# Layer two's residual: LayerNorm scale and offset applied by GpSimd during the input projection and kept in DRAM, in a two-layer RWKV-7 / MLA / gMLP step on Trainium2

## The chip, the cores and the metric

The kernel runs on one core of one Trainium2 chip. The metric is the device time of one execution in microseconds (us). The time before is the median of three executions; the profile is of one more execution.

## What is computed

One inference step of a backbone of two post-norm layers over 1152 tokens (1024 latent, 128 context), width 1024. Cut to what matters here:

```python
for layer in (0, 1):
    h   = x * (1 + scale1) + shift1                  # modulated input
    z   = h @ w_in                                   # input projection: RWKV | MLA (q, kv, rope) | gMLP
    y   = concat(rwkv7(z), mla(z), gmlp(z))
    mix = y @ w_out
    x   = layer_norm(ALPHA * x + gate1 * mix, ln1_g, ln1_b)       # the residual ALPHA * x
    ff  = swiglu(x * (1 + scale2) + shift2, ffn_w_in, ffn_w_out)
    x   = layer_norm(ALPHA * x + gate2 * ff, ln2_g, ln2_b)
```

`layer_norm` is `(x - mean) * rsqrt(var + eps) * g + b`. At the end of layer one the kernel stores only the normalised rows, without `ln2_g` and `ln2_b`. Where layer two needs `ALPHA * x` as its residual, it has to put both back: `xhat * (ALPHA * ln2_g) + ALPHA * ln2_b`. That pair of operations is what the change is about.

## The kernel before

Tokens are nine tiles of 128 rows (`NT` = 9), and three blocks of 384 columns where tokens run along the free dimension. Every fp32 product is three matmuls of split operands (high by high, high by low, low by high; `mm3`, L115 to L121), so each operand is split into a high and a low tile (`split`, L125 and L126; weights in `split_w`, L321 and L324). The Tile framework puts the instructions into an order for each engine and adds the waits: a tile of a pool that takes memory which an earlier pool had waits for whatever still uses that memory. Engines and DMA queues work strictly in their order. DMAs are issued from three queues: SP (`nc.sync`), ACT (`nc.scalar`) and POOL (`nc.gpsimd`).

A layer goes through these stages (`run`, L1515):

1. `project_a` (L344, called at L1541): the 416 columns of `w_in` that MLA reads. Each of the nine token tiles takes 24 matmuls (L360) into one PSUM bank of stream `ps`, which has four banks (`streams`, L1539). A finished bank is copied to a row tile `zrow` and stored to the DRAM tensor `zA`. The pool `zr` with `zrow` opens on the left side just before, and closes just after.
2. `mla_prep` (L579, called at L1549): loads `zA` back as `zt` (L602, SP queue, three buffers), takes RMS norms (ACT L605 and L606, DVE L607 to L613), the rope products on GpSimd (L623 to L626), and transposes on TensorE (L629, L630).
3. The other projections, gMLP, attention and the RWKV scan.
4. `w_out` (L1330): for each tile four products with a quarter of `w_out` (evicted by DVE with the gate, L1352), then `finish` (L1354): the residual is loaded to `xres` (L1363, ACT queue), added to `z` (L1366), normalised (L1304), transposed and modulated to the FFN's input (`to_h`, L284: TensorE L295, ACT L299, DVE L301), then given LN1's scale and offset on GpSimd (L1369, L1370; the last two tiles on DVE) and stored.
5. `ffn` (L1390): first products evicted at L1417 and L1418. Its last part adds the FFN's output to `acc` (GpSimd, L1485), normalises (L1318) and stores the rows as the DRAM tensor that the next layer reads as `self.x` (ACT queue, L1500). At the end of layer one it also makes the modulated input of layer two (`to_h`), the last tiles of which overlap `project_a` of layer two.

Eviction and store in `project_a`, the copy that alternates between ACT and DVE, and the scale and offset rows that `ln_rows` broadcasts to 128 partitions:

```python
            for b in g:
                for j, p in enumerate(ps[b]):
                    z = self.t(tmp, [128, 416], "zrow", bufs=2)
                    self.copy(z, p)                                  # L131 ACT, L133 DVE
                    nc.scalar.dma_start(self.zA[3 * b + j], z)       # L387
...
        gb = self.t(pool, [128, 2, D], tag, bufs=bufs)
        for x, n in enumerate("gb"):                                 # L1299: two DMAs, POOL queue
            nc.gpsimd.dma_start(gb[:, x], self.I[f"{name}_{n}"][l:l + 1].to_broadcast([128, D]))
        if factor is not None:                                       # L1301
            nc.gpsimd.tensor_scalar(gb, gb, factor, None, op0=ALU.mult)
```

In layer two's `w_out`, L1335 makes the rows ALPHA * ln2_g and ALPHA * ln2_b (tile `lnprev`), and `finish` multiplies and adds them on DVE, in place on `xres` (L1364, L1365). Layer one's `w_out` has neither.

Of the kernel before, what the change touches and what calls it, by code (L numbers as in the profile page):

```python
# [11 lines left out]
ALU = mybir.AluOpType  # L12
# [4 lines left out]
D = 1024  # L17
# [4 lines left out]
NT = T // 128  # L22
# [6 lines left out]
ALPHA = (2 * DEPTH) ** 0.25  # L29
# [49 lines left out]
class Net:  # L79
# [1250 lines left out]
    def w_out(self, l, lnp, y, ws, gate, cols, wp):  # L1330

        nc = self.nc
        zp, close_z = self.pool("z", "right")
        gb = self.ln_rows(l, "ln1", zp)
        gp = None if l == 0 else self.ln_rows(l - 1, "ln2", zp, ALPHA, "lnprev")  # L1335
        x1 = self.t(self.dram, [NT, 128, D], "x1", bufs=1)
        self.h2 = {}
        zs = {}

        def product(i, ns):  # L1340
            if i == 8:
                gates.append(self.gate(l, 0, 1, lnp))
            if i not in zs:
                zs[i] = self.t(zp, [128, D], "z", bufs=3) if i % 4 else self.t(wp, [128, D], "z0")
            hh, hl = y[i // 3]
            s = slice(128 * (i % 3), 128 * (i % 3) + 128)
            for n in ns:
                wh, wl = ws[n]
                w = slice(256 * n, 256 * n + 256)
                p = self.psum()  # L1350
                self.mm3(p[:, 0:256], [(hh[:, k, s], hl[:, k, s], wh[:, k], wl[:, k]) for k in (6, 7, 0, 1, 2, 3, 4, 5)])
                nc.vector.tensor_tensor(zs[i][:, w], p[:, 0:256], gates[-1][:, w], op=ALU.mult)  # L1352

        def finish(i):  # L1354
            if i % 3 == 0:
                self.h2[i // 3] = self.hy()
            z = zs[i]
            x = self.t(lnp, [128, D], "xres")
            if l == 0:
                nc.scalar.dma_start(x, self.x_tile(i))  # L1360
                nc.vector.scalar_tensor_tensor(z, x, ALPHA, z, op0=ALU.mult, op1=ALU.add)
            else:
                nc.scalar.dma_start(x, self.x[i])  # L1363
                nc.vector.tensor_tensor(x, x, gp[:, 0], op=ALU.mult)  # L1364
                nc.vector.tensor_tensor(x, x, gp[:, 1], op=ALU.add)  # L1365
                nc.vector.tensor_tensor(z, z, x, op=ALU.add)  # L1366
            self.normalise(z, lnp)
            self.to_h(i, z, self.h2[i // 3], cols, lnp, eng=nc.vector, act=True)
            (nc.vector if i > 6 else nc.gpsimd).tensor_tensor(z, z, gb[:, 0], op=ALU.mult)  # L1369
            (nc.vector if i > 6 else nc.gpsimd).tensor_tensor(z, z, gb[:, 1], op=ALU.add)  # L1370
            nc.scalar.dma_start(x1[i], z)
        gates = [gate]

        for i in range(3):
            product(i, range(3))
        for i in range(NT):
            product(i, [3] if i < 3 else range(4))
            finish(i)
        close_z()
        self.x = x1  # L1380
# [134 lines left out]
    def run(self):  # L1515
        nc = self.nc
# [5 lines left out]
        xp, close = self.pool("x0", "right")  # L1522
# [14 lines left out]
                self.to_h(i, xs[i], self.h[i // 3], self.mod_cols(0, 0), xp, 6, (4 * e,) if g[0] == 0 else (0, 4))  # L1537
        for l in range(self.depth):
            self.streams(ps="0123", bg="67", mp="45")  # L1539
            zp, close_z = self.pool("zr", "left")  # L1540
            self.project_a(l, zp, *(() if l else (first_ada, rows)))  # L1541
            close_z()
# [69 lines left out]
            xp, close_x = self.pool("wx", "right")  # L1612
# [61 lines left out]
```

## Time and profile before

| | |
|---|---|
| three executions | 3696.85, 3701.43, 3705.38 us; median 3701.43 us |
| profiled execution, its own time | 3698.82 us (span 3697.0 us) |
| TensorE (PE) busy | 3486.4 us, 94% of the span |
| VectorE (DVE) busy | 1881.7 us, 51% |
| GpSimd (POOL) busy | 1436.8 us, 39% |
| ScalarE (ACT) busy | 1099.0 us, 30% |
| mean granted clock of TensorE | 0.968 |

PE is TensorE's matmuls, PEld its weight loads, SP the engine that only issues DMAs. ACTq, SPq and POOLq are an engine's issuing of DMAs. Times of the trace are microseconds from the start of the span. A name such as `zrow<-b` is "tile written <- tile read", with buffer numbers left out; `b` is a PSUM bank. An arrow in brackets names what ended the engine's idle time before that row. The chain of waits is the chain of work that ended last, followed back from the last instruction. Idle time of an engine that is not on that chain costs nothing.

### The profile page before, as it was taken

Reading aid. Unit: us, or ns where it says so; the run is one execution under the profiler, and the core shown is the slowest. Engines: PE = TensorE matmul, PEld = TensorE weight load, DVE = VectorE, ACT = ScalarE, POOL = GpSimd, SP = SyncE. Lnnn points to the kernel's source line nnn. Section 1 sums busy time; section 2 is a strip of 40 time slices with the busy share of each in tenths; the row PEclk is TensorE's granted clock in tenths of the full one; section 3 lists DMA queues with packets and bytes.
Section 4 is the critical chain, followed back from the end, with each engine's and each line's share of the span. In section 5 each row is a group of like instructions: output and inputs, shape, how many; then the busy total and the mean of one; then the engine's idle time right before and its main releaser. Section 6 shows DMA issues by size and latency. Waiting matters only on the chain.

```text
span 3697.0 us, 61363 instructions
## 1 busy us (share of the span) xinstructions
PE 3486.4 (94%) x25199; PEld 3030.5 (82%) x25199; DVE 1881.7 (51%) x3064; ACT 1099.0 (30%) x2156; POOL 1436.8 (39%) x1315
## 2 busy tenths in 40 slices
PE   8999789997999999999999997999988999999997
PEld 6888566776988888988989895777778999999996
DVE  3554676755733333333465457767458233433357
ACT  3443344333411111111144434544334211111111
POOL 2324677664411111111453247766634111111146
PEclk9999799998999999999999998989999999999998
DMA  7566545435232222212234654644343111111122
GB/s 288 164 205 171 121 103 135 87 77 167 104 97 91 80 80 80 69 58 69 100 110 118 206 148 106 134 104 96 80 163 110 46 35 46 46 35 46 46 86 80
DMA packets 462584, 387.11 MB, mean 105 GB/s; under 512 B 170412, under 2 KB 394024, under 8 KB 461088
## 3 DMA queue, kind: packets, MB, share of 16 engines
q1 hardware_dynamic: 371744, 249.12, 23.8%
q10 hardware_dynamic: 82176, 113.70, 10.0%
q0 software_dynamic: 8384, 20.38, 1.9%
q8 instruction: 198, 3.24, 0.4%
q14 instruction: 82, 0.67, 0.1%
HBM read 280.10 MB, written 103.02 MB: 104 GB/s over the span
## 4 chain that ended last, share of the span: by engine, by line
PE 72%; DVE 11%; DMA 7%; POOL 4%; issue 3%; ACT 2%; SPq 1%; ACTq 0%; POOLq 0%; DVEq 0%
PE b L119 19%; PE b L121 19%; PE b L120 19%; PE b L360 2%; DVE pr_x L1125 2%; PE b L874 2%; PE b L247 2%; DMA szin<-sd 1%; DVE mx L747 1%; PE b L411 1%; POOL acc L854 1%; DVE hyl L126 1%; PE b L742 1%; DMA wr<-in_w_out_dram 1%; DMA qd<-qo 1%
## 5 line engine op out<-in xcount | busy, mean ns | idle before, releaser
L121 PE MATMUL b<-hyh,w 128*128 128x384 f32 x2544 | 858.0, 337 | 0.0
L119 PE MATMUL b<-hyh,w 128*128 128x384 f32 x2448 | 823.4, 336 | 0.0
L120 PE MATMUL b<-hyl,w 128*128 128x384 f32 x2448 | 822.5, 336 | 0.0
L324 POOL TENSOR_TENSOR w<-wr,w 128x2048 fp32r<-128x2048 f32 x64 | 296.2, 4628 | 1187.1 <-ACT w L321 986.9
L121 PEld LDWEIGHTS b<-hyh,w 128*128 128x128 f32 x2544 | 478.4, 188 | 24.0 <-issue 23.3
L119 PEld LDWEIGHTS b<-hyh,w 128*128 128x128 f32 x2448 | 460.4, 188 | 21.1 <-issue 20.0
L120 PEld LDWEIGHTS b<-hyl,w 128*128 128x128 f32 x2448 | 460.4, 188 | 9.8 <-issue 8.3
L1418 DVE TENSOR_TENSOR fs<-fs,b 128x384 f32<-128x384 f32 x132 | 72.9, 553 | 627.4 <-PE b L121 622.1
L854 POOL TENSOR_TENSOR acc<-acc,P 128x512 f32<-128x512 f32 x224 | 304.0, 1357 | 89.9 <-ACT P L769 81.9
L321 ACT CAST w<-wr 128x2048 fp32r<-128x2048 f32 (+2 forms) x86 | 161.2, 1874 | 586.5 <-PE b L120 517.5
L120 PE MATMUL b<-w,hidh 128*128 128x512 f32 x756 | 299.5, 396 | 0.0
L121 PE MATMUL b<-w,hidl 128*128 128x512 f32 x756 | 299.4, 396 | 0.0
L119 PE MATMUL b<-w,hidh 128*128 128x512 f32 x756 | 298.3, 396 | 0.0
L126 DVE TENSOR_TENSOR hidl<-fs,hidh 128x384 fp32r<-128x384 f32 x126 | 230.6, 1832 | 81.3 <-ACT hidh L125 79.2
L1432 DVE TENSOR_TENSOR acc<-acc,b 128x512 f32<-128x512 f32 x288 | 191.5, 684 | 139.3 <-PE b L121 139.3
L769 ACT ACTIVATE P<-b 128x512 f32<-128x512 f32 x288 | 170.4, 601 | 194.2 <-PE b L121 154.3
L747 DVE TENSOR_REDUCE mx<-b 128x1 f32<-128x512 f32 x256 | 167.9, 681 | 89.6 <-PE b L742 88.6
L119 PE MATMUL b<-w,hyh 128*128 128x256 f32 x576 | 167.9, 293 | 24.2 <-ACT w L321 19.5
L125 ACT CAST hidh<-fs 128x384 fp32r<-128x384 f32 x126 | 64.3, 511 | 397.8 <-DVE fs L1418 397.8
L1417 ACT ACTIVATE fs<-b 128x384 f32<-128x384 f32 x132 | 64.9, 493 | 372.3 <-PE b L121 357.3
L119 PEld LDWEIGHTS b<-w,hidh 128*128 128x128 f32 x756 | 142.1, 188 | 35.1 <-issue 1.7
L121 PEld LDWEIGHTS b<-w,hidl 128*128 128x128 f32 x756 | 142.1, 188 | 34.3
(436 smaller groups left out, 7014.4 us busy)
## 6 DMA issues: line engine op xcount, KB each, us to landing
wr<-in_ffn_w_in_dram SPq DMA_DIRECT2D x88, 512.0 KB, 4.7
fx<-in_ada_w_dram SPq DMA_DIRECT2D x28, 1024.0 KB, 5.1
wr<-in_ffn_w_out_dram SPq DMA_DIRECT2D x22, 1024.0 KB, 4.9
wr<-in_ada_w_dram SPq DMA_DIRECT2D x20, 1024.0 KB, 9.0
qT<-qd ACTq DMA_DIRECT2D x32, 448.0 KB, 4.6
zin<-zd SPq DMA_DIRECT2D x36, 384.0 KB, 5.7
xres<-x ACTq DMA_DIRECT2D x27, 512.0 KB, 3.5
wr<-in_w_in_dram SPq DMA_DIRECT2D x12, 1024.0 KB, 6.6
```

What stands on the lines that cost most here:

```text
L119: mm(out, ah, bh, start=(i == 0), stop=False)
L120: mm(out, ah, bl, start=False, stop=False)
L121: mm(out, al, bh, start=False, stop=(i == n - 1))
L126: (lo_eng or self.nc.vector).tensor_tensor(lo, src, hi.bitcast(F32), op=ALU.subtract)
L247: nc.tensor.matmul(p[32 * jj:32 * jj + 32, :], self.sc[:, 2 * jj + e, :], w[:, 2 * j + e, :], start=(e == 0), stop=(e == 1), tile_position ...
L321: self.nc.scalar.copy(hi, r)
L324: (eng or self.nc.gpsimd).tensor_tensor(lo[:, s], r[:, s], hi[:, s].bitcast(F32), op=ALU.subtract)
L360: nc.tensor.matmul(p, x[:, 4 * e + k, s], y[:, k], start=(e + k + n == 0), stop=(e == 1 and k == 3 and n == 2))
L747: nc.vector.tensor_reduce(mx[:, i, c:c + 1], p, axis=AX.X, op=ALU.max)
L769: nc.scalar.activation(P[:, 0:nq], p[:, 0:nq], AF.Exp, scale=MLA_SCALE)
L854: nc.gpsimd.tensor_tensor(acc, Ps[0] if k == 1 else acc, P, op=ALU.add)
L1432: nc.vector.tensor_tensor(acc[i][:, w], acc[i][:, w], p, op=ALU.add)
```

## The change

In layer two only, the multiply and the add of `lnprev` leave `w_out`. Before `project_a` a pool `gp` opens on the left side. It takes the two rows of `lnprev` and two buffers `xp`. For each of the nine tiles: load the stored rows on the SP queue, multiply and add on GpSimd, store to a new DRAM tensor `xr` on the SP queue. The pool closes, the pool `zr` opens, and `w_out` later loads its residual from `xr`.

```diff
@@ w_out
         gb = self.ln_rows(l, "ln1", zp)
-        gp = None if l == 0 else self.ln_rows(l - 1, "ln2", zp, ALPHA, "lnprev")
@@ finish, in w_out
                 nc.scalar.dma_start(x, self.x[i])
-                nc.vector.tensor_tensor(x, x, gp[:, 0], op=ALU.mult)
-                nc.vector.tensor_tensor(x, x, gp[:, 1], op=ALU.add)
                 nc.vector.tensor_tensor(z, z, x, op=ALU.add)
@@ run
             self.streams(ps="0123", bg="67", mp="45")
+            if l:
+
+                gpp, close_g = self.pool("gp", "left")
+                gp = self.ln_rows(l - 1, "ln2", gpp, ALPHA, "lnprev")
+                xr = self.t(self.dram, [NT, 128, D], "xr")
+                for i in range(NT):
+                    x = self.t(gpp, [128, D], "xp", bufs=2)
+                    nc.sync.dma_start(x, self.x[i])
+                    nc.gpsimd.tensor_tensor(x, x, gp[:, 0], op=ALU.mult)
+                    nc.gpsimd.tensor_tensor(x, x, gp[:, 1], op=ALU.add)
+                    nc.sync.dma_start(xr[i], x)
+                self.x = xr
+                close_g()
             zp, close_z = self.pool("zr", "left")
             self.project_a(l, zp, *(() if l else (first_ada, rows)))
             close_z()
```

In the changed kernel the new lines are L1544 (load of `xp`), L1545 (multiply), L1546 (add) and L1547 (store of `xr`); lines outside the new block are named here by their number before the change.

Three places of the program show what moved. The number after a name tells one tile from another; what stands in brackets is what the instruction waits for, by engine or DMA queue (DMAHW: hardware queues of SP and ACT, DMASW: POOL's queue).

ScalarE where `project_a` of layer two begins to evict, before:

```order
L125 CAST hyh_17009<-hf_17148 128x4x128 [waits Activation_49]
L125 CAST hyh_17009<-hf_17160 128x4x128 [waits Activation_49]
L131 COPY zrow_17264<-b_2646_17189 128x416 [waits PE_49]
L387 DMA zA_68<-zrow_17264 128x416 [waits DMAHW4_49,Activation_49]
L605 ACTIVATE ckf_17466,ss_17465<-zt_17463 128x256 [waits DMAHW5_49,DMAHW6_49,DMAHW3_49,DMAHW7_49,DMAHW2_49,DMAHW0_49]
```

The same place now:

```order
L125 CAST hyh_17009<-hf_17160 128x4x128 [waits Activation_49]
L131 COPY zrow_17318<-b_2657_17243 128x416 [waits DMAHW2_49,DMAHW3_49,DMAHW1_49,DMAHW4_49,DMAHW0_49,DMAHW5_49,DMASW6_49,DMAHW6_49,DMASW5_49,DMAHW7_49,PE_49,Pool_49]
L387 DMA zA_68<-zrow_17318 128x416 [waits Activation_49]
L387 DMA zA_68<-zrow_17321 128x416 [waits DVE_49]
L131 COPY zrow_17324<-b_2659_17245 128x416 [waits DMAHW6_49,PE_49]
```

The first `zrow` copy waited for TensorE alone; now it also waits for GpSimd, both POOL loads and eight hardware DMA queues, and `zt`'s first squares (L605) come later in ScalarE's order.

The SP queue at the same place, before:

```order
L314 DMA wr_17177<-in_w_in_dram 128x4x416 [waits DMAHW7_49,DMAHW0_49,Pool_49]
L314 DMA wr_17183<-in_w_in_dram 128x4x416 [waits DMAHW1_49,DMAHW0_49,DVE_49]
L314 DMA wr_18312<-in_w_in_dram 128x8x256 [waits DMAHW2_49,DMAHW1_49,DVE_49]
L602 DMA zt_17463<-zA_68 128x416 [waits DMAHW4_49,DMAHW5_49,DMAHW3_49,DMAHW6_49,DMAHW0_49,DMAHW7_49,PE_49,Activation_49]
L602 DMA zt_17493<-zA_68 128x416 [waits DMAHW6_49]
L602 DMA zt_17523<-zA_68 128x416 [waits DMAHW2_49,DMAHW0_49]
```

The end of the new transfers there now:

```order
L1544 DMA xp_17212<-x_2533_16559 128x1024 [waits DMAHW6_49,DMAHW0_49]
L1544 DMA xp_17217<-x_2533_16559 128x1024 [waits DMAHW7_49,DMAHW1_49]
L1547 DMA xr_17181<-xp_17212 128x1024 [waits Pool_49]
L1547 DMA xr_17181<-xp_17217 128x1024 [waits Pool_49]
L1544 DMA xp_17222<-x_2533_16559 128x1024 [waits DMAHW4_49,DMAHW2_49]
L1547 DMA xr_17181<-xp_17222 128x1024 [waits DMAHW5_49,Pool_49]
L602 DMA zt_17517<-zA_68 128x416 [waits DMAHW0_49,DMAHW6_49,PE_49,Activation_49]
L602 DMA zt_17547<-zA_68 128x416 [waits DMAHW7_49]
```

All eighteen transfers of `xp` and `xr` now stand ahead of the first `zt` load, in pairs: two loads, two stores, two loads.

GpSimd from the last split of layer two's input to the first new operations, now (before, nothing of `lnprev` or `xp` stood here):

```order
L126 TENSOR_TENSOR hyl_17010<-hf_17148,hyh_17009 128x4x128 [waits DVE_49,Activation_49]
L1545 TENSOR_TENSOR xp_17182<-xp_17182,lnprev_17177 128x1024 [waits DMAHW2_49,Pool_49]
L1545 TENSOR_TENSOR xp_17187<-xp_17187,lnprev_17177 128x1024 [waits DMAHW3_49]
L1546 TENSOR_TENSOR xp_17182<-xp_17182,lnprev_17177 128x1024 [waits Pool_49]
L1546 TENSOR_TENSOR xp_17187<-xp_17187,lnprev_17177 128x1024 [waits Pool_49]
L1545 TENSOR_TENSOR xp_17192<-xp_17192,lnprev_17177 128x1024 [waits DMAHW6_49,DMAHW0_49,Pool_49]
```

The eighteen new operations stand behind the last `hyl` split and go in pairs of tiles; the two loads of `lnprev` and its scaling (L1301) stand a little earlier, behind the last addition to `acc`, and are gone from `w_out`.

## Rows read from the trace of the kernel before

**Rows 1.** The page: the span, each engine's busy time, the chain's shares.

```profile
span 3697.0 us, 61363 instructions
...
PE 3486.4 (94%) x25199; PEld 3030.5 (82%) x25199; DVE 1881.7 (51%) x3064; ACT 1099.0 (30%) x2156; POOL 1436.8 (39%) x1315
...
PE 72%; DVE 11%; DMA 7%; POOL 4%; issue 3%; ACT 2%; SPq 1%; ACTq 0%; POOLq 0%; DVEq 0%
```

**Rows 2.** The chain at layer two's `project_a`: start us, us, what.

```profile
1919.04 36.26 PE b L360 x192
1955.30 0.34 PE b L629 x3
```

**Rows 3.** ScalarE's timeline there: start us, us, engine line operation [idle before].

```profile
1923.61 0.51 ACT L131 COPY zrow<-b 128x416 f32<-128x416 f32 x1 [1.59 <-PE b L360]
...
1929.00 0.42 ACT L605 ACTIVATE ckf<-zt 128x256 f32<-128x256 f32 x1 [4.89 <-DMA zt<-zA]
```

**Rows 4.** The chain at layer two's `w_out`.

```profile
2733.73 9.81 DMA lnprev<-in_ln_b_dram
...
2743.70 5.40 POOL lnprev L1301
```

**Rows 5.** GpSimd's timeline at layer two's `project_a`.

```profile
1905.37 1.28 POOL L1485 TENSOR_TENSOR acc<-acc,fs 128x512 f32<-128x512 f32 x1
...
1919.61 0.60 POOL L589 DMA_DIRECT2D ropek<-in_k_ropek_dram  x1 [2.86 <-DMA wr<-in_w_in_dram]
...
1922.31 0.54 POOL L397 DMA_DIRECT2D rw_a<-in_rw_a_dram  x1
...
1923.04 1.31 POOL L126 TENSOR_TENSOR hyl<-hf,hyh 128x512 fp32r<-128x512 f32 x1
```

**Rows 6.** GpSimd's timeline in layer two's `w_out`.

```profile
2770.36 2.38 POOL L1369 TENSOR_TENSOR z<-z,lngb 128x1024 f32<-128x1024 f32 x1 [3.36 <-PE b L295]
2772.82 2.40 POOL L1370 TENSOR_TENSOR z<-z,lngb 128x1024 f32<-128x1024 f32 x1
```

**Rows 7.** GpSimd's groups there (2723.2 to 2860.1): busy us, mean ns.

```profile
L1370 POOL TENSOR_TENSOR z<-z,lngb 128x1024 f32<-128x1024 f32 x7 | 19.9, 2837 | 0.3
```

**Rows 8.** DMA issues of the whole run: KB each, median us from issue to landing.

```profile
xres<-x ACTq DMA_DIRECT2D x27, 512.0 KB, 3.5
...
szin<-sd SPq DMA_DIRECT2D x18, 512.0 KB, 4.7
...
x<-acc ACTq DMA_DIRECT2D x9, 512.0 KB, 2.6
...
zt<-zA SPq DMA_DIRECT2D x18, 208.0 KB, 2.5
```

**Rows 9.** TensorE's timeline: the first matmuls after an idle stretch.

```profile
2703.57 1.01 PE L119 MATMUL b<-w,hyh 128*128 128x256 f32 x3 [5.27 <-ACT w L321]
```

**Rows 10.** One window: us, PE, PEld, DVE, ACT, POOL busy, PEclk, DMA, GB/s.

```profile
2703.57:2707.16 3.59, 3.59 (x17) 3.59 (x18) 2.27 (x1) 0.92 (x1) 0.38 (x2) 0.50 0.60 184
```

**Rows 11.** DVE's groups in layer two's `w_out`: busy us, mean ns, idle before.

```profile
L1364 DVE TENSOR_TENSOR xres<-xres,lnprev 128x1024 f32<-128x1024 f32 x9 | 19.0, 2116 | 6.9 <-DMA xres<-x 5.3 <-POOL lnprev L1301 1.6
L1365 DVE TENSOR_TENSOR xres<-xres,lnprev 128x1024 f32<-128x1024 f32 x9 | 11.0, 1220 | 0.1
```

**Rows 12.** DVE's timeline: `w_out`'s first eviction, FFN's third, layers one and two.

```profile
888.53 1.01 DVE L1352 TENSOR_TENSOR z<-b,gate 128x256 f32<-128x256 f32 x3
...
1019.72 0.56 DVE L1418 TENSOR_TENSOR fs<-fs,b 128x384 f32<-128x384 f32 x1 [3.64 <-PE b L121]
...
2723.22 1.09 DVE L1352 TENSOR_TENSOR z<-b,gate 128x256 f32<-128x256 f32 x3 [0.90 <-PE b L121]
...
2868.11 0.56 DVE L1418 TENSOR_TENSOR fs<-fs,b 128x384 f32<-128x384 f32 x1 [2.92 <-PE b L121]
```

**Rows 13.** Windows over `w_out` in layers one and two, columns as Rows 10.

```profile
888.53:1011.60 123.07, 119.37 (x941) 118.58 (x942) 85.35 (x139) 49.10 (x88) 49.70 (x29) 0.99 0.36 125
2723.20:2860.10 136.90, 120.69 (x920) 118.37 (x920) 110.36 (x155) 48.52 (x87) 57.87 (x30) 0.96 0.32 111
```

**Rows 14.** DVE's timeline at `project_a` of layer two: the first `zt` tile done.

```profile
1931.09 0.28 DVE L613 TENSOR_SCALAR zt<-zt,ss 128x128 f32<-128x128 f32 x1
```

## The prediction, on record before the changed kernel ran

> **What bounds the kernel now.** The page comes first: TensorE is busy for 94% of the span and holds 72% of the chain of waits; GpSimd is busy for 39% and holds 4% [rows 1]. GpSimd has room over the whole span, so the question is only where its new work lands. That takes the chain and the timelines at the two places that the change touches.
>
> At the first place, layer two's `project_a`, the chain is TensorE alone: 192 of the 216 L360 matmuls in 36.26 us, 0.189 us each, and the first transposes of `mla_prep` (L629) follow at once, at 1955.30 [rows 2]. The loads of `zt`, its squares and the `zrow` copies lie beside that [rows 3] and cost nothing. So the stage is free of GpSimd, and any pause of TensorE in it lengthens the run one for one.
>
> At the second place, layer two's `w_out`, the chain goes through the load of `lnprev` (9.81 us) and its scaling on GpSimd (5.40 us) before `xres` can be multiplied [rows 4]. Here the removed work does stand on the path, in part.
>
> **The change, part by part.** The order of the instructions shows that the new GpSimd pass does not run beside the projection. Pool `zr` takes the memory of the closed pool `gp`, so the first `zrow` copy waits for the whole pass and its last store. TensorE has four `ps` banks. It fills four of the nine tiles, which is 96 of the 216 matmuls, and the first matmul of the fifth tile waits for a `zrow` copy. Of the 96, 24 are done before the 192 of the chain; so TensorE stops at 1919.04 + 72 × 0.189 = 1932.6.
>
> When does the pass end?
>
> - Start. GpSimd's last addition to `acc` ends at 1905.37 + 1.28 = 1906.65 [rows 5]. Then come two `lnprev` loads: two issues at 0.53 (between the 0.60 and 0.54 of its other issues [rows 5]) and 9.81 to the landing, as in `w_out` [rows 4], make 1917.5. The scaling takes 5.4: 1922.9. Behind it on GpSimd stand a `hyl` split (1.3), six DMA issues that take 3.2 now (1919.61 to 1922.85), and the last `hyl` split (1.3) [rows 5]. The first new operation starts at about 1928.7. The first two `xp` loads have long landed by then, since the ScalarE queue has stored the rows of their tiles.
> - One operation. The nearest row is GpSimd's own tensor-tensor at 128x1024, in place with a row tile: 2.38 and 2.40 us where nothing disturbs it [rows 6], 2.84 in the mean of L1370 beside a busy VectorE [rows 7]. VectorE waits during the pass, so I take 2.40, with 2.84 as the upper end.
> - One pair of tiles. Four operations are 9.6. The two buffers make it longer: the first tile's store is issued after the third operation (7.2), lands 2.6 later as a 512 KB store of rows does, and only then its buffer's next load can go, 3.5 for such a load [rows 8]: 13.3 us a pair. With 2.84 and the 4.7 of the slowest-landing 512 KB load in rows 8 it would be 8.5 + 2.6 + 4.7 = 15.8.
> - The end. Four pairs, then the ninth tile's two operations and its store: 1928.7 + 4 × 13.3 + 4.8 + 2.6 = 1989.3. The `zrow` copy takes 0.51 [rows 3], so the first bank is free at 1989.8.
>
> TensorE therefore stands idle from 1932.6 to 1989.8, 57.2 us. The 120 matmuls left take 22.7 at 0.189. After the idle the clock is likely to be low first: after 5.27 us without a matmul [rows 9] the next 3.59 us ran at a granted 0.50, the level of 1.2 GHz, though TensorE was busy throughout [rows 10]. That is 1.8 lost; I add 2. L360 ends at 1989.8 + 22.7 + 2 = 2014.5 in place of 1955.3: **+59.2 us**. Nothing gives it back: the next stage needs all nine `zA` tiles, and its `zt` loads stand on the SP queue behind the last `xr` store. ScalarE and VectorE wait in `zrow` copies meanwhile, with `mla_prep` and the weight splits behind them; nobody is waiting for those but the idle TensorE. The first `zt` tile then takes about 2 + 2.5 + 2.4 after its copy, and is ready while the remaining matmuls run. The eighteen DMAs are 9.4 MB on a queue that carries nothing urgent then.
>
> The row says 2.40 us for an operation on 1024 elements a partition [rows 6]. The Trainium skill, "GPSIMD Engine Reference", section "Elementwise — side-by-side cycle accounting", gives 4497 ns for a fp32 tensor-tensor add over 2048 elements, 1.96 times VectorE's time, and speaks against moving such work to GpSimd. By an estimate from that page an operation would be 2.25 us, a pair's first three 6.75, and the sum some 2 us smaller; the trace agrees within 7%, and the row is used.
>
> The gain in `w_out`. VectorE loses nine multiplies (19.0 us busy) and nine additions (11.0) [rows 11], and the head loses the `lnprev` wait. What of these 30 us was on the path is read from layer one, whose `w_out` is the same code without both: from the first product's eviction to the third of the FFN it takes 1019.72 - 888.53 = 131.2 us, in layer two 2868.11 - 2723.22 = 144.9 [rows 12]. The windows say the same, 123.1 against 136.9 with TensorE busy for about 120 in both [rows 13]. So **-13.7 us**. The ends: 8, if part of layer two's loss is its colder clock (0.96 against 0.99 [rows 13]) and late weights rather than VectorE; 20, if most of the removed 30 us was on the path. The nine loads of `xres` stay, from `xr`, which was stored some 700 us earlier.
>
> Sum: 3698.82 + 59.2 - 13.7 = 3744.3 for an execution like the profiled one. The median shown is 3701.43, 2.6 above that execution, so I predict **3747 us**, 1.2% slower.
>
> **The rivals.**
>
> - *A longer pass.* The same mechanism with the upper prices: 4 × 15.8 + 5.7 + 2.6 = 71.5 for the pass in place of 60.6, so 3758. For it speaks that both operations read two SBUF tiles while loads and stores run; against, that VectorE is idle then.
> - *The bank hold is loose, the queue holds.* If the first `zrow` copies get through before the pass ends, TensorE finishes L360 as now, and `mla_prep` waits for `zt` behind the last `xr` store, issued at 1986.7. A `zt` load takes 2.5 [rows 8] and its norm 2.4 (from 1929.00 [rows 3] to 1931.37 [rows 14]): L629 at 1991.6, +36.3, with 2 for the clock. 3698.8 + 36.3 + 2 - 13.7 + 2.6 = 3726. Against it stands the copy's own list of waits.
> - *It does what it says (faster).* The pass lies beside the projection and TensorE never lacks a bank, which needs the release by 1932.6; only the gain of `w_out` is left: 3698.8 - 13.7 + 2.6 = 3688. The point at which gain and loss cancel is a release 13.7 us later, near 1946. From 1928.7 that leaves 17.6 us for eighteen operations, under 1 us each without any round trip, where the rows say 2.40. It could only be if the waits listed for the copy were met long before by other work.
>
> **How the numbers follow.** Bank hold at about my prices 0.73, its own range 3736 to 3754 (the ends of the gain, and a few us of the pass); longer pass 0.14; queue alone 0.08; faster 0.05. The range takes in the first three, from the queue alone (3726) to the longer pass with a gain of only 8 us in `w_out` (3764), and on both sides the 4 us by which the three executions shown lie off their median: **3722 to 3768**. Outside are the faster case and about 0.1 for waits that no row shows. A measurement of this kernel can tell about 0.2%, 7.4 us, from no change. Faster by more 0.05, within it 0.02, slower 0.93.
>
> **What would show it.** Right: in `project_a` of layer two a gap of TensorE of about 57 us from near 1933, ended by a `zrow` copy; that copy released by the last store of `xr`; nine pairs of L1545 and L1546 at about 2.4 us in a rhythm of 13 us per two tiles, with GpSimd waiting for `xp` loads between; L360's end near 2014; no `lnprev` in `w_out`, and its stretch near 131 us. Wrong: a gap under 20 us; a pass that starts before 1920 or runs without pauses between pairs (9.6 a pair, which would take 15 us off); GpSimd operations near 1.3 or over 3.5 us; or a `w_out` that stays at 145 us, which would mean that late weights and not the two VectorE operations set its pace.

## The result: 1.3% slower, by the hold that was forecast

The changed kernel takes 3747.19 us (median), the kernel before 3699.14 us: a ratio of 1.0132, 95% interval 1.0114 to 1.015. The median is over four executions, of which one ran in a slower state (4950.99 us at a granted clock of 0.634) that the ratio leaves out; the other three lie at 3744.39 to 3748.37 us. The kernel before has a fourth execution now, so its median is 2.3 us below the one shown ahead of the change. The profiled execution took 3744.39 us with a span of 3742.6 us. The page of the changed kernel answers to [rows 1]; the fence has the span, the engines' busy time and the chain's shares:

```profile
span 3742.6 us, 61414 instructions
...
PE 3486.5 (93%) x25199; PEld 3029.7 (81%) x25199; DVE 1875.7 (50%) x3046; ACT 1098.1 (29%) x2156; POOL 1476.2 (39%) x1333
...
PE 71%; DVE 10%; DMA 7%; POOL 5%; issue 3%; ACT 3%; SPq 1%; ACTq 0%; POOLq 0%; DVEq 0%
```

TensorE has the same work (3486.5 us busy against 3486.4) in a span that is 45.6 us longer. VectorE lost its eighteen operations (30 us busy [rows 11]), but only 6 us of busy time, since others of its operations took longer; the last section shows the longest. The busy shares say nothing of where the 45.6 us are. The waits between 1915 and 2013 do. This view of the changed kernel lists who waited for whom: us in total, times, longest:

```profile
ACT zrow L131 <- DMA xr<-xp: 64.2, 1, 64.2
...
PE b L360 <- ACT zrow L131: 56.7, 1, 56.7
...
POOL xp L1545 <- DMA xp<-x: 18.1, 4, 4.9
```

Read upwards from TensorE: one wait of 56.7 us, for a `zrow` copy; that copy waited 64.2 us for the last store of `xr`; and GpSimd waited four times for loads of `xp`. TensorE's timeline shows the two edges of the gap:

```profile
1930.53 0.35 PE L360 MATMUL b<-w,hyl 128*128 128x416 f32 x1
1987.56 1.06 PE L360 MATMUL b<-w,hyh 128*128 128x416 f32 x2 [56.67 <-ACT zrow L131]
```

The chain through the same stretch (start us, us, what) replaces the 36.26 us of plain matmuls of [rows 2]:

```profile
1924.34 4.69 POOL xp L1545 x2
1929.04 4.63 POOL xp L1546 x2
1933.69 2.84 DMA xr<-xp
1936.54 3.04 DMA xp<-x
...
1979.40 2.35 POOL xp L1545
1981.82 2.35 POOL xp L1546
1984.18 2.56 DMA xr<-xp
1987.00 0.52 ACT zrow L131
1987.56 25.08 PE b L360 x120
2012.63 0.34 PE b L629 x3
```

Between one pair of tiles and the next lie a store and, behind it, a load. The ninth tile's store lands, the copy runs, and the remaining 120 matmuls follow at once.

The gain is in `w_out`. Its start is marked here by the last reciprocal of attention (L784), its end by the third eviction of the FFN (L1418 before, L1415 after the change moved the lines). VectorE's timeline, first of the kernel before, then of the changed one:

```profile
2701.02 0.95 DVE L784 RECIPROCAL rc<-b 64x128 f32<-64x128 f32 x1 [0.61 <-POOL o L785]
```

```profile
2759.71 0.95 DVE L784 RECIPROCAL rc<-b 64x128 f32<-64x128 f32 x1 [0.61 <-POOL o L785]
...
2913.70 0.55 DVE L1415 TENSOR_TENSOR fs<-fs,b 128x384 f32<-128x384 f32 x1 [3.11 <-PE b L121]
```

With the end before at 2868.11 [rows 12], the stretch takes 167.09 us before and 153.99 us now: 13.1 us less. The account of the two profiled executions closes. From the first L360 of layer two (at 1901.59 before, 1900.18 now) to the first transpose L629 (1955.13 and 2012.47) 53.54 us became 112.29, which is +58.75. From there to the reciprocal (745.89 and 747.24) +1.35. In `w_out` -13.1. Ahead of all that -1.4. Sum +45.6, the difference of the spans.

### The profile page after: what moved, and what is told of

Read it like the earlier page. It is cut to its first block, busy times and chain, and to the rows that moved or that the text cites. A ratio compares the mean times of both kernels' runs of the same rounds, so it can differ in the third digit from the quotient of the medians.

```text
span 3742.6 us, 61414 instructions
## 1 busy us (share of the span) xinstructions
PE 3486.5 (93%) x25199; PEld 3029.7 (81%) x25199; DVE 1875.7 (50%) x3046; ACT 1098.1 (29%) x2156; POOL 1476.2 (39%) x1333
## 4 chain that ended last, share of the span: by engine, by line
PE 71%; DVE 10%; DMA 7%; POOL 5%; issue 3%; ACT 3%; SPq 1%; ACTq 0%; POOLq 0%; DVEq 0%
PE b L119 19%; PE b L121 19%; PE b L120 19%; PE b L874 2%; PE b L360 2%; PE b L247 2%; DVE pr_x L1125 2%; DMA szin<-sd 1%; DVE mx L747 1%; PE b L411 1%; POOL acc L854 1%; PE b L742 1%; DVE hyl L126 1%; DMA wr<-yd 1%; DMA qd<-qo 1%
## 5 line engine op out<-in xcount | busy, mean ns | idle before, releaser
L119 PEld LDWEIGHTS b<-hyh,w 128*128 128x128 f32 x2448 | 460.1, 188 | 21.1 <-issue 20.0
L1415 DVE TENSOR_TENSOR fs<-fs,b 128x384 f32<-128x384 f32 x132 | 72.8, 553 | 627.8 <-PE b L121 622.7
L874 PE MATMUL b<-P,vt 128*64 128x256 f32 x1152 | 171.3, 415 | 1.9 <-ACT P L769 1.7
```

The lines of the kernel that those rows point to most:

```text
L119: mm(out, ah, bh, start=(i == 0), stop=False)
L874: nc.tensor.matmul(po[0][64 * i:64 * i + 64, 0:256], vt[:, k], Ps[k][:, 256 * i:256 * i + 256], start=(k == 0), stop=(k == 9))
```

## The experiments

The theory at this point: the first `zrow` copy waits for memory that the pass uses, and nothing else about the pass costs much. The main rival: the pass costs its time wherever it lies, through GpSimd's and the SP queue's order. The kernels ran in three groups, each beside the kernel before on the same chip (medians 3696.86, 3701.61 and 3703.32 us), so results are given as ratios to that. Where a time was expected, it was meant against about 3697; a ratio times 3697 is what to hold against it. Single traces of the same code differ: up to its `w_out`, e15_pool_wout has the work of the kernel before, but needs 807.6 us from the first L360 to the reciprocal where the kernel before took 799.4. So differences of a few us are read from the ratios, not from one trace.

**Own place.** The pool is kept until the projection is done:

```diff
                 self.x = xr
-                close_g()
             zp, close_z = self.pool("zr", "left")
             self.project_a(l, zp, *(() if l else (first_ada, rows)))
             close_z()
+            if l:
+                close_g()
```

> Pool gp stays open until project_a is done, so zrow has memory of its own; nothing else is edited. Theory (the 57 us are the zrow copies waiting for memory that the pass uses): the gap of 56.7 us in TensorE goes, the w_out gain of about 13 us stays, and what is left of the pass costs 0 to 12 us beside mla_prep, so 3686 to 3700 us. Rival (the pass costs its time wherever it lies, by the SP queue and GpSimd's own order, which hold zt and the rope products): first transposes of mla_prep near 1990, 3715 to 3730 us.

Measured: 3721.28 us, ratio 1.0067 (1.0054 to 1.008). Neither side is right alone. The hold is gone: project_a takes 54.1 us from the first L360 to the first L629 (1896.04 to 1950.1), near the 53.5 before. But the time lies in the rival's range: 0.99% over the kernel without the pass (next experiment) are left, about 37 us. They lie behind project_a, in `mla_prep`. The same stretch of some 160 matmuls from the first L629 on, in e1_own_place and in e2_gain_only (us, then PE busy and its matmuls; the granted clock is the first number behind POOL's brackets):

```profile
1950.10:2011.30 61.20, 34.86 (x162) 29.93 (x161) 40.37 (x82) 18.33 (x68) 51.41 (x71) 0.69 0.52 177
```

```profile
1950.30:1976.30 26.00, 26.00 (x161) 25.53 (x160) 16.53 (x48) 12.99 (x42) 13.35 (x33) 1.00 0.50 159
```

That is 35.2 us: 26.3 of idle TensorE and 8.9 more of busy time at the lower granted clock. TensorE's waits there, GpSimd's timeline at the longest of them, and two rows of VectorE right behind it, all of e1_own_place:

```profile
PE b L629 <- DVE zt L612: 20.2, 7, 7.7
PE b L629 <- DVE zt L613: 3.3, 2, 1.7
```

```profile
1987.47 2.34 POOL L1545 TENSOR_TENSOR xp<-xp,lnprev 128x1024 f32<-128x1024 f32 x1
1989.76 1.37 POOL L141 TENSOR_TENSOR ss<-ss,mhalf 128x2 f32<-128x2 f32 x2
1991.09 2.35 POOL L1546 TENSOR_TENSOR xp<-xp,lnprev 128x1024 f32<-128x1024 f32 x1
1993.40 2.39 POOL L1545 TENSOR_TENSOR xp<-xp,lnprev 128x1024 f32<-128x1024 f32 x1
```

```profile
1991.17 2.42 DVE L612 TENSOR_SCALAR zt<-zt,ss 128x256 f32<-128x256 f32 x1
1993.51 2.36 DVE L613 TENSOR_SCALAR zt<-zt,ss 128x128 f32<-128x128 f32 x1
```

Three things make the `zt` tiles late. The RMS norm takes its reciprocal root on GpSimd (L141), and that root, like the rope products, now stands between operations of 2.34 us. VectorE's operations beside them take longer: L612 and L613 took 2.42 and 2.36 us here, and 0.35 and 0.28 in the median of the kernel before. And `zt` loads come late: of the longest wait, 7.7 us up to 1990.91, L1545 accounts for 2.3, and ahead of that ScalarE's squares (L605) had waited for a `zt` load until 1985.94; what held that load is not separated. With the wait for memory gone, these were the next waits in line.

**The gain alone.** No pass at all, and w_out adds the stored rows as they are (the three lines of the change in w_out and finish, without the block in run). It leaves scale and offset out, so it does not compute the step; it serves to measure.

> Leaves out the scale and the offset of layer two's residual altogether: no pass, no lnprev, w_out adds the stored rows as they are. Theory (the removal is worth the 13.1 us that the stretch of w_out got shorter): 3684 to 3690 us. Rival (the stretch got shorter for another reason, a shifted clock or weights that arrive earlier after the pause): within 6 us of the kernel before.

Measured: 3683.73 us, ratio 0.9968 (0.9955 to 0.998), 13.1 us by the medians and 12 by the ratio. In its trace the stretch of `w_out` takes 156.25 us (2696.34 to 2852.59), 10.8 less than before. The gain that the trace of the change showed is the removal's own, within 2 or 3 us.

**The loss alone.** The pass as in the change, but w_out as before:

```diff
+            if l:
+                gpp, close_g = self.pool("gp", "left")
...
+                close_g()
             zp, close_z = self.pool("zr", "left")
```

> The kernel before with the pass added as the change adds it, but w_out still loads the old rows and keeps lnprev and its two VectorE operations; what the pass stores is not read. Theory (gain and loss are separate): the gap of 57 us and an unchanged w_out, 57 to 60 us over the kernel before, 3756 to 3760 us. Rival (the pause lets the weights of later stages come early and gives part back): under 3750 us.

Measured: 3756.0 us, ratio 1.0174 (1.0153 to 1.0195), 59.1 us by the medians; its single times spread over 3744.64 to 3768.44. Its trace has the gap (56.2 us of waiting for `zrow`) and a stretch of `w_out` of 164.72 us. 59.1 less 13.1 is 46.0, and the change is 48 us by its medians; by the ratios it is 1.74% less 0.32%, and 1.32%. Within the spread, loss and gain add up.

**Four buffers.** One number: `"xp", bufs=4`.

> The change with four xp buffers in place of two. Theory (4.3 to 4.9 us of each of four round trips through DRAM are part of the hold): GpSimd runs its eighteen operations without a pause, 42.2 us from 1924.3, the first zrow copy comes near 1969 in place of 1987, 3727 to 3731 us. Rival (the round trips are hidden or the DMAs slow down when four buffers are in flight): over 3740 us. Beside it, VectorE's last hyl split, which took 11.39 us in the change and ended 0.6 us after GpSimd's first four operations: if GpSimd's operations on SBUF keep it out until they pause, it takes 18 to 42 us here; if it is slow for another reason, about 11.

Measured: 3733.77 us, ratio 1.0098 (1.0083 to 1.0113). TensorE's wait in project_a, and the first operations of the pass on GpSimd:

```profile
PE b L360 <- ACT zrow L131: 41.5, 1, 41.5
```

```profile
1915.94 5.70 POOL L1301 TENSOR_SCALAR lnprev<-lnprev 128x2048 f32<-128x2048 f32 x1
...
1926.17 9.33 POOL L1545 TENSOR_TENSOR xp<-xp,lnprev 128x1024 f32<-128x1024 f32 x4
1935.46 9.22 POOL L1546 TENSOR_TENSOR xp<-xp,lnprev 128x1024 f32<-128x1024 f32 x4
```

The gap shrank by 15.2 us, where 18 were expected. From its first operation to the `zrow` copy (1971.27) the pass took 45.1 us, against 62.7 in the change: 17.6 less, so the round trips are what was claimed. But the pass began 1.9 us later, because here `lnprev`'s scaling came behind another `hyl` split. The result lies between the two expectations, nearer the theory's. On VectorE's `hyl` split it tells nothing: here it ran at 1919.98, ahead of the pass.

**VectorE in GpSimd's place.** e1_own_place with `nc.vector` for the two operations.

> Pool gp keeps its own place as in e1_own_place, and VectorE does the eighteen operations in place of GpSimd (1.22 us each in the row of w_out before, so 22 us in all). It tells what the 37 us are that e1_own_place still takes over e2_gain_only. Theory (GpSimd's order: the rsqrt of mla_prep and the rope products stand behind operations of 2.34 us, and TensorE's transposes wait for them): most of the 37 us go, 3684 to 3700 us. Rival (the SP queue, where zt loads stand behind xr stores and xp loads, which stay as they are): 3710 us or more.

Measured: 3697.68 us, ratio 0.9994 (0.9981 to 1.0007). TensorE's wait for `zt` in mla_prep is down to a single one:

```profile
PE b L629 <- DVE zt L612: 1.5, 1, 1.5
```

Of the 0.99% that e1_own_place had over e2_gain_only, 0.73 are gone, some 27 of 37 us. So most of it came from GpSimd doing the work; about 10 us were something else. Of the three ways seen in e1_own_place this run tells nothing apart: it takes GpSimd's long operations away, and with them what stood behind them, what ran slowly beside them, and the late `zt` loads.

**The pass after mla_prep.** The block of the change, moved behind `self.mla_prep(l)`, its pool closed behind it.

> The pass as in the change (GpSimd, SP queue, two buffers, pool closed behind it), but written after mla_prep, so that not zr but the pools of the next projections open in its place. Theory (what opens in the place of the closed pool waits for the whole pass): the hold moves on, project_a has no gap, and the first zraw copies of the next projections wait instead; TensorE finds only mla_prep's own work meanwhile, 3715 to 3760 us. Rival (the hold was special to project_a's four banks, and later stages have slack): 3684 to 3700 us.

Measured: 3760.75 us, ratio 1.0164 (1.0144 to 1.0184), which is 3758 us against 3697, at the upper end of the theory's range. The gain of w_out is in this figure too, so the pass costs over 70 us here. Two waits can be seen. The first is the hold, one stage later: the last store of `xr` on the chain of e6_after_prep, ScalarE's first `zraw` copy of the next projections (1961.70 in the kernel before), and the matmul that waited for it:

```profile
2056.67 3.29 DMA xr<-xp
```

```profile
2060.54 0.87 ACT L459 COPY zraw<-b 128x384 f32<-128x384 f32 x2
```

```profile
2061.08 0.44 PE L119 MATMUL b<-hyh,w 128*128 128x384 f32 x1 [0.24 <-ACT zraw L459]
```

The copy follows 0.6 us after the store has landed. TensorE had left these projections at 1972.28 and takes them up again here; in between it did the work that stands next in its order, and waited for that. The second wait is for late `zt` tiles again (29.7 us of waits of L629 for L612, one of them for an L612 that took 4.73 us). Another 14.7 us it waited for the key-value weights, whose load (L651) GpSimd issued at 2019.48, between two operations of the pass. What each is worth is not separated. TensorE is nearly empty in two of these stretches, as the windows show (us, then PE busy and its matmuls; the granted clock is the first number after the brackets):

```profile
1975.00:2000.00 25.00, 4.54 (x18) 2.90 (x18) 14.68 (x36) 6.02 (x28) 20.98 (x31) 0.51 0.32 102
2000.00:2025.00 25.00, 1.46 (x6) 0.64 (x4) 6.03 (x12) 2.14 (x10) 20.33 (x16) 0.50 0.52 181
```

**Late and small.** Quarters of 256 columns, tied to a late value by the scalar that scales them, in a pool that stays:

```diff
+        al = self.t(gpp, [128, 1], "al")
+        nc.gpsimd.tensor_scalar(al, late, 0.0, ALPHA, op0=ALU.mult, op1=ALU.add)
+        for h in range(4):
...
+            nc.gpsimd.tensor_scalar(gp, gp, al, None, op0=ALU.mult)
+            for i in range(NT):
+                x = self.t(gpp, [128, 256], "xp", bufs=2)
```

> The pass in four column quarters (256 columns, lnprev and two buffers together 4 KB per partition in place of 16), its scaling tied to the last split of the key-value weights in mla_prep, where GpSimd stood idle for 40 us in the kernel before, and a pool of its own until the projections are done. Theory (the pass is free where no released memory and no operation of the chain stands behind it): 3684 to 3694 us, as without the pass. Rival (72 small transfers on the SP queue and 72 operations get in the way there as well): 3700 us or more.

Measured: 3829.27 us, ratio 1.0347 (1.0329 to 1.0364), the worst of all and a plain miss. GpSimd's waits between 2010 and 2240, and its groups between 2010 and 2190:

```profile
POOL xp L594 <- DMA xp<-x: 66.0, 22, 6.5
```

```profile
L594 POOL TENSOR_TENSOR xp<-xp,lnprev 128x256 f32<-128x256 f32 x36 | 27.8, 780 | 66.3 <-DMA xp<-x 66.0
L595 POOL TENSOR_TENSOR xp<-xp,lnprev 128x256 f32<-128x256 f32 x36 | 27.0, 760 | 1.3
```

A quarter of the columns costs a third of the time per operation, but a whole round trip through DRAM per pair of pieces (up to 6.5 us). The pass lasted from 2015.83 to 2177.5, far past the 40 idle us that it was meant for, into the query projection, whose work on GpSimd and whose loads stood behind it: TensorE was busy for 14 to 21 of 40 us in the windows from 2080 to 2200. Which of the two queues held it there was not separated.

**GpSimd in w_out.** The kernel before with `nc.gpsimd` for L1364 and L1365.

> The kernel before with the multiply and the add of lnprev left in w_out, but on GpSimd in place of VectorE; no pass and no new transfers. Theory (of the 13 us that the removal gives, VectorE's share comes back, but the wait for lnprev stays and the rsqrt of each tile stands behind 4.7 us of GpSimd work): within 10 us of the kernel before, either way. Rival (VectorE's 30 us were the whole matter): 3684 to 3690 us.

Measured: 3730.14 us, ratio 1.0076 (1.0054 to 1.0098), which is 28 us: slower than either side expected. TensorE's waits in w_out, where the kernel before has 11.9 us of this wait:

```profile
PE b L295 <- ACT z L1318: 30.2, 6, 11.8
```

From the reciprocal to the third eviction it takes 188.46 us, 21.4 more than with VectorE. The expected reason does not show: in seven of the nine tiles GpSimd stood idle before the root of the layer norm (L141), for 21.1 us in all, waiting for VectorE. What grew are operations of VectorE beside GpSimd's. One tile of e15_pool_wout, GpSimd and then VectorE, with the same L1315 one tile later where GpSimd was idle:

```profile
2777.36 0.57 POOL L141 TENSOR_TENSOR lrs<-lrs,mhalf 128x1 f32<-128x1 f32 x1 [1.37 <-DVE lrs L1313]
2777.90 2.34 POOL L1364 TENSOR_TENSOR xres<-xres,lnprev 128x1024 f32<-128x1024 f32 x1
```

```profile
2777.96 2.29 DVE L1315 SCALAR_TENSOR_TENSOR lrs<-lmv,lrs 128x1 f32<-128x1 f32 x1 [0.68 <-POOL lrs L141]
...
2792.36 0.16 DVE L1315 SCALAR_TENSOR_TENSOR lrs<-lmv,lrs 128x1 f32<-128x1 f32 x1 [0.66 <-POOL lrs L141]
```

L1315 stands between the root and the copy to `z` (L1318) that TensorE waits for. Its median is 2.29 us here and 0.15 before; that of the addition of `xres` (L1366) is 3.25 us and 1.22. On the chain of this run stand four of these long L1315 and six long L1366.

**Four buffers for VectorE, and another queue.** e16_own_vector with four buffers; and the same with the loads and stores of the pass on the POOL queue.

> e16_own_vector (own place, VectorE) with four xp buffers in place of two, still on the SP queue. It tells whether the 10 us that e16_own_vector keeps over e2_gain_only lie in the round trips of two buffers (VectorE and the zt loads behind it on the SP queue wait for them). Theory (they do): 3684 to 3692 us, at least 0.2% under the kernel before. Rival (they lie in the 23 us of VectorE work itself, in a stage where VectorE also splits weights): 3693 to 3702 us.

> As e17_vector_four, but the loads of xp and the stores of xr are issued from the POOL queue in place of the SP queue, so that no zt or weight load stands behind them. Theory (the SP queue holds what is left): at or under e17_vector_four, 3684 to 3692 us. Rival (a store that waits for VectorE now stops GpSimd, and with it the rsqrt of mla_prep): slower than e17_vector_four by 3 us or more.

Measured: 3695.76 us, ratio 0.9979 (0.9969 to 0.999), and 3692.9 us, ratio 0.9979 (0.9967 to 0.9991): 3689 us against 3697, in the theory's range. Both beat the kernel before, by 0.21%, and the change by 1.5%. The four buffers bring about 0.15% over e16_own_vector, so the round trips were probably a part of its 10 us; the intervals overlap. The queue makes no difference that shows. Some 0.11% lie between these two and e2_gain_only, about 4 us, with overlapping intervals as well; whether that is VectorE's 22 us of work (eighteen operations of 1.22) in a stage where it also splits weights stays open.

## Why the prediction was right, point by point

- *The hold.* The copy waits for the whole pass and its last store, TensorE stops with four banks full, nobody else is the cause: shown by the wait of 64.2 us, by e1_own_place, where the gap goes with the one edit of where the pool closes, and by e6_after_prep, where the copies of the pool that opens next wait for the last store. The gap was forecast as 57.2 us and is 56.7.
- *The start of the pass.* Forecast 1928.7, measured 1924.28. 1.4 of the 4.4 us is that the whole trace was that much earlier; the rest is the term for the load of `lnprev`, taken as 9.81 us to landing from w_out, while here the second load landed 6.99 us after its issue (1906.13 to 1913.12).
- *One operation.* Taken as 2.40 us, measured 2.32 in pairs (4.63 for two), so the upper end of 2.84 did not come about. VectorE ran nothing beside most of the pass, as argued; only beside the first four operations it had a split that was held (last section).
- *One pair.* Taken as 13.3 us, measured 13.8 (1924.28 to 1979.40 in four pairs). The three operations to the first store took 7.0 to 7.1 us, and that store held up the next load for 2.7, as taken. The term that was too small is the load: 3.9 to 4.4 us from its issue to GpSimd's next operation, for 3.5. The second load of a pair lands while the first tile's multiply runs. SP's queue and GpSimd behind the first pair:

```profile
1931.40 2.61 SPq L1547 DMA_DIRECT2D xr<-xp  x2
1934.10 2.77 SPq L1544 DMA_DIRECT2D xp<-x  x2
```

```profile
1937.99 4.63 POOL L1545 TENSOR_TENSOR xp<-xp,lnprev 128x1024 f32<-128x1024 f32 x2 [4.33 <-DMA xp<-x]
```

Four times 0.5 us on the one side and 3 us on the other at the start: the end came at 1987.0 for a forecast of 1989.3. Errors of a few us cancel here (the gap also began 1.7 us early, at 1930.88), which is luck, not method.
- *The clock.* 2 us added; the 120 matmuls took 25.08 us instead of 22.7, and the window of them shows a granted clock of 0.91. This is near the size of [rows 10].

```profile
1987.50:2012.60 25.10, 25.04 (x122) 24.59 (x123) 5.77 (x13) 5.04 (x13) 3.17 (x10) 0.91 0.30 93
```

- *The gain.* -13.7 us from the comparison with layer one. By the marks of the prediction, from the first eviction of `w_out` (2783.41 now) to the third of the FFN, it is 130.29 us for a forecast of 131.2, so -14.6; from the reciprocal on, -13.1; in e2_gain_only 11 to 13. The comparison of two stages with the same code, one with and one without the operations, was worth more than the 30 us of busy time.
- *Sum.* +59.2 and -13.7 forecast, +58.75 and -13.1 measured, 3747 against 3747.19 us. The mechanism and its size were right; the agreement to 0.2 us is luck.
- *The rivals.* The longer pass did not come about. The queue rival (the hold is loose, later waits cost about 36 us all the same) was not the case in the change, but e1_own_place shows that a loss of the same size was next in line: with the hold removed, 37 us stay. That the two sizes agree is chance. In the prediction all of `mla_prep` came late behind the last `xr` store; in e1_own_place it began on time, and late `zt` loads were only one of three ways in which its tiles came late.

## What to carry to other kernels

A pool that closes in front of another one is an edge in the schedule: whatever opens in its place waits for its last reader, here for a store whose tensor was first read 779 us later. Before an engine with idle time is given work, list what stands behind that work on its queue, and what runs beside it on other engines; GpSimd was 39% busy, yet a reciprocal root of 0.6 us stood behind its operations of 2.34 in one stage, and VectorE's operations beside them took 2 us longer in two, so the idle time was not free in any stage that was tried. And what a removed operation was worth is read best from a stage with the same code without it.

## What was not expected of the hardware

VectorE's last `hyl` split, an operation with two inputs in SBUF, took 11.39 us in the change, 6.31 in e1_own_place and 0.69 in e4_four_buffers, where it ran ahead of the pass. VectorE's rows, in that order of the kernels:

```profile
1922.83 11.39 DVE L126 TENSOR_TENSOR hyl<-hf,hyh 128x512 fp32r<-128x512 f32 x1 [1.18 <-ACT hyh L125]
```

```profile
1921.52 6.31 DVE L126 TENSOR_TENSOR hyl<-hf,hyh 128x512 fp32r<-128x512 f32 x1 [1.18 <-ACT hyh L125]
```

```profile
1919.98 0.69 DVE L126 TENSOR_TENSOR hyl<-hf,hyh 128x512 fp32r<-128x512 f32 x1 [1.77 <-ACT hyh L125]
```

It ends at 1934.22 in the first. GpSimd's `hyl` split, two multiplies and two additions ran without a pause from 1923.04 to 1933.66; the VectorE operation ended 0.56 us behind the last of them. In the second a `hyl` split and two multiplies of GpSimd ended at 1927.27 and VectorE's operation at 1927.83, 0.56 us again, while GpSimd's next operation (L623) took 0.71 us, where it takes 0.25 to 0.30 later in that run. So it was not held for one GpSimd operation, but for five and for three in a row. The Trainium skill, "SBUF — State Buffer", section "SBUF: two separate sides", says that a VectorE instruction with two SBUF inputs and a GpSimd instruction that reads SBUF contend for a shared port pair, and that the later one is blocked until the first has finished. The first half agrees with these rows; the second is too short here, where the block lasted over five GpSimd operations, though VectorE's row begins 0.21 us ahead of GpSimd's first. No run of this study took the contention away by itself, so its cause is inferred from the coinciding times, here and in the longer L612, L613 and L1315 of e1_own_place and e15_pool_wout, which each end within 0.2 us of the GpSimd operation beside them. Whether L612 and L613, which read one tile and a column of scalars, are held for the same reason stays open. The held split cost the change nothing, since TensorE stood still, but held time counts as busy: the page of e2_gain_only, without the pass, has VectorE busy for 1862.6 us, 13 less than the change, and 10.7 of these 13 are this one operation.
